# The last four output tiles of a streaming encoder's final FFN: kept weight halves and an end taken 144 frames at a time

## The chip, the cores and the metric

The kernel runs on one core of a Trainium2 chip. The metric is the device time of one execution in microseconds (us). The time before is 2776.94 us, the median of three runs (2775.93 to 2778.15). Five engines work side by side, each on its own instruction queue: PE multiplies matrices, DVE, ACT and POOL work element by element on 128 partitions, SP issues most of the DMAs.

## The reference

One inference step of a two-layer encoder on 256 prompt frames and 32 sample frames, model width 2048. Layer 0 mixes frames with a gated MLP, layer 1 with multi-scale retention; each mixer is followed by a SwiGLU FFN of hidden width 5632. Only the last lines matter here:

```python
def layer_norm(x, g, b):
    mu = jnp.mean(xf, axis=-1, keepdims=True)
    var = jnp.mean(jnp.square(xf - mu), axis=-1, keepdims=True)
    y = (xf - mu) * lax.rsqrt(var + LN_EPS) * g.astype(jnp.float32) + b.astype(jnp.float32)
...
        x = layer_norm(ALPHA * x + h, ln_mix_g[i], ln_mix_b[i])
        x = layer_norm(ALPHA * x + swiglu(x, w_ffn_in[i], w_ffn_out[i]), ln_ffn_g[i], ln_ffn_b[i])
```

The mean and the variance of one frame run over all 2048 channels. So no channel of a frame can be normalised before the last of the 16 channel tiles of that frame is known.

## The kernel before

**Layout.** Activations are held transposed: 128 channels on the partitions, the 288 frames (NT) along the free axis. A matrix of 2048 output channels is 16 output tiles `m` (KT = 16); the FFN's hidden width is 44 tiles, done in two halves of 22 (HH).

**One product in three.** Every float32 operand is split into a high part and a low part (`split`: an ACT cast, L450, then a DVE subtraction, L451). `Core.step` issues three matmuls per block of 128 x 128 weights: high weights on high data (L105), high weights on low data (L106), low weights on high data (L107), all into one PSUM bank of 288 columns. `halves` writes the access pattern of a moving operand: four elements of the second half of the frames, four of the first, and so on backwards.

**Weights.** They come from HBM in chunks of eight blocks (512 KB). `Core.prep` issues the DMA of a chunk on SP's queue into one of three `raw` buffers, casts it into one of four `whi` buffers and subtracts into one of four `wlo` buffers. A `raw` buffer is free for the next DMA when the subtraction has read it, a `whi` or `wlo` buffer when the last matmul of its chunk has read it. `Core.blk` hands out a block and calls `prep` three chunks ahead.

**Order.** PE's order is the order of the program text. DVE's and ACT's order is chosen by a planner, except inside a `manual_schedule` block with FINISH, where DVE, ACT and POOL run in the order of the text as well.

**The last stage.** `ffn` of layer 1 computes `f_out` of its second half with `Core.tiles`: output tile after output tile, 22 blocks of three matmuls each. After each tile `PostNorm.last` adds the bank to `y` (L246); `sums` subtracts a centring row (L295), squares on ACT (L297) and adds both to running sums (L300, L301). After the last tile `stats` (L307) forms mean and mean square by matmuls with a matrix of 1/2048 (L313, L316), and `finish` (L329) does the rest: variance (L373), its power -1/2 by a logarithm and an exponential on ACT (L374, L375), one Newton step (L377 to L379), then for each pair of tiles of `y` a centring and a scaling (L345; on POOL for tiles 4, 5 and 8 to 11), for four tiles a centring by PE into PSUM (L369, L370) with the scaling on DVE (L352), then the affine map with gain and bias of the channel (ACT, L362, or DVE, L360), and a store (L363). PE's constants for the centring, `ident` and `minus`, live in a `raw` buffer called `centring`, taken when 15 tiles are done.

## Time and profile before

| what | value |
|---|---|
| median of three runs | 2776.94 us |
| profiled execution, its time | 2776.59 us |
| profiled execution, its span | 2774.8 us |
| PE busy | 2762.4 us, 100% of the span |
| DVE, ACT, POOL busy | 1696.9, 1247.2, 141.6 us |

The span is the time from the first to the last instruction of the program in the profile; the run's time holds 1.8 us more. A row of the timeline gives start, duration, engine, line, operation, output and input with their shapes, and in brackets how long the engine had been idle and what ended the wait. Rows of the same kind in a row are merged ("x11" is eleven instructions). PEld is PE's weight load, which overlaps its matmuls.

### The profile page before, as it was taken

What the parts mean: (1) busy time and instruction counts of PE and PEld (TensorE: products, weight loads), DVE (VectorE), ACT (ScalarE), POOL (GpSimd) and SP (SyncE); (2) the same over time, 40 slices, a digit from 0 to 9 for tenths busy, and PEclk for the clock granted to TensorE, in tenths of its full rate; (3) what the DMA queues carried; (4) which work ended last, traced back from release to release, by engine and by line L of the source; (5) the groups of instructions that cost most, each with busy time, mean ns of one, the idle gap of its engine ahead of it and who ended that gap; (6) DMA issues with size and microseconds to landing.
All of it is one profiled execution on the core that took longest, in us unless ns stands there. A gap on an engine that the chain in (4) does not pass through costs nothing.

```text
span 2774.8 us, 51493 instructions
## 1 busy us (share of the span) xinstructions
PE 2762.4 (100%) x21590; PEld 2750.3 (99%) x21590; DVE 1696.9 (61%) x2468; ACT 1247.2 (45%) x1659; POOL 141.6 (5%) x241
## 2 busy tenths in 40 slices
PE   9999999999999999999999999999999999999998
PEld 9999999999999999999999999999999999999998
DVE  6688964445444466867765666767854455444465
ACT  5455554333343344645443444445643333333343
POOL 1100000000000000012200121210000000000001
PEclk9999999999999999999999999999999999999999
DMA  8655555555555555567765666765555555555553
GB/s 285 212 185 166 170 176 172 173 174 175 175 171 173 178 174 178 171 213 240 231 201 175 196 216 219 222 204 171 173 171 172 174 175 175 172 172 174 174 175 126
DMA packets 146585, 515.51 MB, mean 186 GB/s; under 512 B 18016, under 2 KB 20336, under 8 KB 146320
## 3 DMA queue, kind: packets, MB, share of 16 engines
q1 hardware_dynamic: 131984, 473.47, 52.6%
q0 software_dynamic: 14224, 38.59, 4.6%
q8 instruction: 169, 2.77, 0.4%
q14 instruction: 64, 0.52, 0.1%
q10 hardware_dynamic: 144, 0.15, 0.0%
HBM read 486.98 MB, written 25.17 MB: 185 GB/s over the span
## 4 chain that ended last, share of the span: by engine, by line
PE 99%; DVE 0%; DMA 0%; ACT 0%; issue 0%; SPq 0%; DVEq 0%
PE af_in L107 13%; PE af_in L105 13%; PE af_in L106 13%; PE ab_in L105 7%; PE ab_in L107 7%; PE ab_in L106 7%; PE af_out L105 6%; PE af_out L106 6%; PE af_out L107 6%; PE ab_out L105 2%; PE aa_in L106 2%; PE aa_in L105 2%; PE aa_in L107 2%; PE ab_out L107 2%; PE ab_out L106 2%; PE aa_out L106 1%
## 5 line engine op out<-in xcount | busy, mean ns | idle before, releaser
L451 DVE TENSOR_TENSOR wlo<-raw,whi 128x1024 fp32r<-128x1024 f32 (+1 forms) x892 | 1084.8, 1218 | 856.1 <-ACT whi L450 848.7
L450 ACT CAST whi<-raw 128x1024 fp32r<-128x1024 f32 (+1 forms) x892 | 933.7, 1049 | 1325.5 <-PE af_in L106 325.8
L105 PE MATMUL af_in<-xh,whi 128*128 128x288 f32 (+1 forms) x2816 | 813.3, 289 | 0.0
L107 PE MATMUL af_in<-xh,wlo 128*128 128x288 f32 (+1 forms) x2816 | 813.2, 289 | 0.0
L106 PE MATMUL af_in<-xl,whi 128*128 128x288 f32 x2816 | 811.9, 288 | 0.0
L106 PEld LDWEIGHTS af_in<-xl,whi 128*128 128x128 f32 x2816 | 528.1, 188 | 0.0
L105 PEld LDWEIGHTS af_in<-xh,whi 128*128 128x128 f32 x2816 | 528.1, 188 | 0.0
L107 PEld LDWEIGHTS af_in<-xh,wlo 128*128 128x128 f32 x2816 | 528.0, 188 | 0.0
L105 PE MATMUL ab_in<-xh,whi 128*128 128x288 f32 (+1 forms) x1536 | 445.2, 290 | 0.0
L107 PE MATMUL ab_in<-xh,wlo 128*128 128x288 f32 (+1 forms) x1536 | 444.0, 289 | 0.0
L106 PE MATMUL ab_in<-xl,whi 128*128 128x288 f32 x1536 | 443.8, 289 | 0.0
L107 PE MATMUL af_out<-hh,wlo 128*128 128x288 f32 x1408 | 406.1, 288 | 0.0
L105 PE MATMUL af_out<-hh,whi 128*128 128x288 f32 x1408 | 406.0, 288 | 0.0
L106 PE MATMUL af_out<-hl,whi 128*128 128x288 f32 x1408 | 406.0, 288 | 0.0
L106 PEld LDWEIGHTS ab_in<-xl,whi 128*128 128x128 f32 x1536 | 288.3, 188 | 0.9
L105 PEld LDWEIGHTS ab_in<-xh,whi 128*128 128x128 f32 x1536 | 288.2, 188 | 0.8
L107 PEld LDWEIGHTS ab_in<-xh,wlo 128*128 128x128 f32 x1536 | 288.2, 188 | 0.0
L105 PEld LDWEIGHTS af_out<-hh,whi 128*128 128x128 f32 x1408 | 264.0, 188 | 0.0
L107 PEld LDWEIGHTS af_out<-hh,wlo 128*128 128x128 f32 x1408 | 264.0, 188 | 0.0
L106 PEld LDWEIGHTS af_out<-hl,whi 128*128 128x128 f32 x1408 | 264.0, 188 | 0.0
L105 PE MATMUL aa_in<-xh,whi 128*128 128x288 f32 x512 | 148.1, 289 | 0.4 <-ACT xh L450 0.4
L107 PE MATMUL ab_out<-r_oh,wlo 128*128 128x288 f32 x512 | 147.8, 289 | 0.0
(248 smaller groups left out, 2915.8 us busy)
## 6 DMA issues: line engine op xcount, KB each, us to landing
raw<-in_wpack_dram SPq DMA_DIRECT2D x887, 512.0 KB, 3.4
v_room<-tv POOLq DMA_DIRECT2D x32, 144.0 KB, 4.9
of<-o_room POOLq DMA_DIRECT2D x32, 144.0 KB, 4.8
vw<-v_room POOLq DMA_DIRECT2D x8, 512.0 KB, 6.0
out_st_s_dram<-sso POOLq DMA_DIRECT2D x16, 256.0 KB, 2.7
o_room<-to POOLq DMA_DIRECT2D x8, 512.0 KB, 3.5
out_st_p_dram<-so POOLq DMA_DIRECT2D x16, 256.0 KB, 5.3
y<-in_xT_dram SPq DMA_DIRECT2D x8, 288.0 KB, 5.2
```

What stands on the lines that cost most here:

```text
L105: mm(wide, hi, halves(xh, lead), start=first, stop=False)
L106: mm(halves(ps[:, lead:], 0, lead), hi, halves(xl), start=False, stop=False)
L107: mm(wide, lo, halves(xh, lead), start=False, stop=last)
L450: nc.scalar.copy(hi, f)
L451: nc.vector.tensor_tensor(lo, f, hi.bitcast(F32), ALU.subtract)
```

## The change

It concerns the second half of layer 1's `f_out` alone, tiles 12 to 15, and the end.

- `f_out` runs through tiles 0 to 11 as before. `ending` takes tiles 12 to 15. In a first pass over these tiles it issues two matmuls of 288 columns per block: low weights on all frames of the high data, into a bank `q`, and high weights on the first 144 frames of high and of low data side by side, into a bank `p` (`paired`). So a first pass gives the first 144 frames in full and a third of the work of the other 144. `second` then issues, tile by tile, the missing matmul: high weights on the last 144 frames of high and low data.
- The high weights of these tiles are 11 chunks and stay until then: seven in the rooms of `xh` and `xl`, which layer 1's input no longer needs (`keep`), four in the `whi` buffers.
- The hidden activations' high and low parts lie in one tile `hid`, row by row, the low part 336 elements behind the high one, so that `paired` can step between them.
- `y` and the output are laid out as two halves of 144 frames.
- `ahead` centres the partial tiles 12 to 15 beforehand, and takes the `centring` buffer before the first pass rather than near its end. `stats` and `finish` are replaced for this layer by `means` and `spread`, once for each half of the frames; the power -1/2 is one ACT function of another table in place of two.
- The first half's centring, scaling, affine maps and stores are put, in the order of the text, between the `second` passes; the second half's follow after the last.

The number of matmuls of `f_out` and the bytes of weights are the same.

```diff
+NH = NT // 2
...
+ENDS = 4
+KEPT = ENDS * HH // CB
+SLOT = ROW + 16
...
-            hi = self.wp.tile([P, CB * P], F32R, tag="whi", name=f"whi{c}")
+            hi = self.keep[c] if c in self.keep else self.wp.tile([P, CB * P], F32R, tag="whi", name=f"whi{c}")
...
+def paired(x, k, h):
+
+    n = NH
+    dims = [list(x.ap[0]), [-4, n // 4], [SLOT, 2], [1, 4]]
+    v = x[:, k, h * n:]
+    return bass.AP(tensor=v.tensor, offset=v.offset + n - 4, ap=dims)
+
...
+            self.yh = y.rearrange("p k n -> p (k n)").rearrange("p (h k n) -> p h k n", h=2, n=NH)
...
+    def tile(self, m):
+        return self.y[:, m, :] if self.out is None else self.yh[:, :, m, :]
...
-                self.core.tables("natural_log_exp_and_others")
+                self.core.tables("abs_reciprocal_sqrt_and_small")
...
-    def finish(self, m1, m2):
-
-
-        nc, core, a, mean = self.nc, self.core, self.a, self.b
...
+    def ahead(self, ms):
+        nc = self.nc
+        for m in ms:
+            nc.vector.tensor_tensor(self.tile(m), self.tile(m), self.like(self.c), ALU.subtract)
+        room = self.core.wp.tile([P, CB * P], F32, tag="raw", name="centring", bufs=3)
...
+    def add(self, h, m, ps):
+        y = self.yh[:, h, m, :]
+        for o in (0, NH):
+            self.nc.vector.tensor_tensor(y, ps[:, o:o + NH], y, ALU.add)
+    def square(self, h, m):
+        self.sq = self.tmp(f"sq{h}_{m}")[:, :NH]
+        self.nc.scalar.activation(self.sq, self.yh[:, h, m, :], AF.Square)
+    def gather(self, h, m):
+        s = self.s[:, :, h * NH:(h + 1) * NH]
+        for i, d in enumerate((self.yh[:, h, m, :], self.sq)):
+            self.nc.vector.tensor_tensor(s[:, i, :], s[:, i, :], d, ALU.add)
+    def end(self, h, m, ps):
+        self.add(h, m, ps)
+        self.square(h, m)
+        self.gather(h, m)
+    def first(self, m, ps, both):
+        y = self.tile(m)
+        self.nc.vector.tensor_tensor(y, self.like(both[:, :NT]), y, ALU.add)
+        self.end(0, m, ps)
+    def means(self, h, parts):
+        core, one = self.core, self.cst["one2048"]
+        self.m = [core.bank(f"m{h}{i}")[:, :NH] for i in range(2)]
+        for j, p in enumerate(parts):
+            for m, r in zip(self.m, p):
+                self.nc.tensor.matmul(m, one, r, start=j == 0, stop=j == len(parts) - 1)
+    def sum_rows(self, h):
+        s = self.s[:, :, h * NH:(h + 1) * NH]
+        return s[:, 0, :], s[:, 1, :]
+    def spread(self, h, mids, between):
+        nc, core = self.nc, self.core
+        cols = slice(h * NH, (h + 1) * NH)
+        m1, m2 = self.m
+        self.scale, self.mean = self.a[:, cols], self.b[:, cols]
+        self.ap = ap = core.bank(f"ap{h}")[:, :NH]
+        v = core.bank(f"fin{h}")[:, :NH]
+        t, r = self.tmp(f"t{h}")[:, :NH], self.tmp(f"r{h}")[:, :NH]
+        nc.scalar.activation(t, m1, AF.Square)
+        nc.scalar.copy(self.mean, m1)
+        mids()
+        nc.vector.scalar_tensor_tensor(v, m2, LN_EPS, t, ALU.add, ALU.subtract)
+        nc.scalar.activation(r, v, AF.Abs_reciprocal_sqrt)
+        between()
+        nc.vector.scalar_tensor_tensor(ap, v, -0.5, r, ALU.mult, ALU.mult)
+        nc.vector.tensor_tensor(ap, ap, r, ALU.mult)
+        nc.vector.scalar_tensor_tensor(self.scale, ap, 1.5, r, ALU.add, ALU.mult)
+        nc.scalar.copy(ap, self.scale)
+    def rows(self, h, k, n, eng, op):
+        f = {ALU.subtract: (self.m[0], self.mean), ALU.mult: (self.ap, self.scale)}[op][eng is self.nc.gpsimd]
+        y = self.yh[:, h, k:k + n, :]
+        eng.tensor_tensor(y, y, f.unsqueeze(1).broadcast_to([P, n, NH]), op)
+    def affine(self, h, k, n, eng=None):
+        nc = self.nc
+        for i in range(k, k + n):
+            d = self.yh[:, h, i, :]
+            if eng is None:
+                nc.scalar.activation(d, d, AF.Identity, bias=self.bias(i), scale=self.gain(i))
+            else:
+                eng.tensor_scalar(d, d, self.gain(i), self.bias(i), ALU.mult, ALU.add)
+    def store(self, h, k, n, queue=None):
+        (queue or self.nc.sync).dma_start(self.out[:, h, k:k + n, :], self.yh[:, h, k:k + n, :])
+    def lift(self, h, k, n):
+        mm = self.nc.tensor.matmul
+        off = self.core.accum(f"off{k}")[:, :n * NH].rearrange("p (k n) -> p k n", n=NH)
+        for i in range(n):
+            mm(off[:, i, :], self.ident, self.yh[:, h, k + i, :], start=True, stop=False)
+            mm(off[:, i, :], self.minus, self.mean, start=False, stop=True)
+        return off
+    def ending(self, w, koff, x):
+        core, nc = self.core, self.nc
         mm = nc.tensor.matmul
+        ms = list(range(KT - ENDS, KT))
+        dve, gps = nc.vector, nc.gpsimd
+        self.ahead(ms)
+        hi, ps = {}, {}
+        for m in ms:
+            ps[m] = p, q = core.accum(f"p{m}"), core.accum(f"q{m}")
+            for k in range(HH):
+                hi[m, k], lo = core.blk(w, koff + k, m)
+                mm(halves(q), lo, halves(x[:, k, :NT]), start=k == 0, stop=k == HH - 1)
+                mm(halves(p), hi[m, k], paired(x, k, 0), start=k == 0, stop=k == HH - 1)
+            if m < KT - 1:
+                self.first(m, p, q)
+                core.tick()
+        def second(m, at={}):
+            ps[m] = b = core.accum(f"b{m}")
+            for k in range(HH):
+                mm(halves(b), hi[m, k], paired(x, k, 1), start=k == 0, stop=k == HH - 1)
+                if k in at:
+                    at[k]()
+        def quad(k, eng=dve):
+            self.rows(0, k, 4, eng, ALU.subtract)
+            self.rows(0, k, 4, eng, ALU.mult)
+        def out(k):
+            self.affine(0, k, 4)
+            self.store(0, k, 4)
         with core.tc.manual_schedule(engines=FINISH):
+            self.first(KT - 1, *ps[KT - 1])
+            second(KT - 4, {19: lambda: self.means(0, [self.sum_rows(0)])})
+            self.spread(0, lambda: None, lambda: self.rows(0, 0, 4, dve, ALU.subtract))
+            quad(12, gps)
+            self.end(1, KT - 4, ps[KT - 4])
+            self.rows(0, 0, 4, dve, ALU.mult)
+            out(0)
+            second(KT - 3)
+            quad(4)
+            out(4)
+            self.end(1, KT - 3, ps[KT - 3])
+            second(KT - 2)
+            quad(8)
+            out(8)
+            out(12)
+            self.end(1, KT - 2, ps[KT - 2])
+            second(KT - 1)
+            self.add(1, KT - 1, ps[KT - 1])
+            self.square(1, KT - 1)
+            self.means(1, [self.sum_rows(1), (self.yh[:, 1, KT - 1, :], self.sq)])
+            off = {}
+            def mids():
+                for k in (2, 5, 8):
+                    off[k] = self.lift(1, k, 3)
+                self.rows(1, 12, 4, gps, ALU.subtract)
+            self.spread(1, mids, lambda: self.rows(1, 0, 2, dve, ALU.subtract))
+            self.rows(1, 12, 4, gps, ALU.mult)
+            def lifted(k):
+                y = self.yh[:, 1, k:k + 3, :]
+                dve.tensor_tensor(y, off[k], self.scale.unsqueeze(1).broadcast_to([P, 3, NH]), ALU.mult)
+            lifted(2)
+            self.rows(1, 0, 2, dve, ALU.mult)
+            self.affine(1, 2, 3)
+            self.store(1, 2, 3)
+            lifted(5)
+            self.affine(1, 0, 2)
+            self.store(1, 0, 2)
+            lifted(8)
+            self.rows(1, 11, 1, dve, ALU.subtract)
+            self.rows(1, 11, 1, dve, ALU.mult)
+            self.affine(1, 5, 3)
+            self.store(1, 5, 3)
+            self.affine(1, 9, 3, dve)
+            self.affine(1, 8, 1)
+            self.store(1, 8, 4)
+            self.affine(1, 14, 2, dve)
+            self.affine(1, 12, 2)
+            self.store(1, 12, 4, nc.scalar)
...
+            hid = pool.tile([P, HH, 2 * ROW], F32R, name="hid")[:, :, LEAD:]
+            hh, hl = hid, hid[:, :, SLOT:]
...
+            ends = 0 if out is None or half == 0 else ENDS
+            if ends:
+                room = [t.rearrange("p k r -> p (k r)") for t in (core.wide_l, core.wide_x)]
+                for i in range(KEPT - 4):
+                    o = 56 + (i // 2) * CB * P
+                    core.keep[NCH - KEPT + i] = room[i % 2][:, o:o + CB * P]
+            core.tiles(f"f_out{layer}", half * HH, list(range(HH)), list(range(KT - ends)),
                        lambda k: (hh[:, k, :NT], hl[:, k, :NT]),
                        ln.last if half else ln.part)
+            if ends:
+                ln.ending(f"f_out{layer}", half * HH, hid)
```

More of the change, by code (lines that the diff above doesn't have):

```diff
@@ L57, in __init__ @@
         self.ready = {}
+        self.keep = {}
         self.nprep = 0
@@ L259, in last @@
             r = self.tmp("cen", F32R)
[L260 removed]
+            nc.scalar.copy(self.like(r), self.tile(m))
             self.core.after(2, lambda: self.center(r))
         self.n += 1
[L263 to L270 removed]
         if self.c is None:
@@ L278, in last @@
                 split(nc, hi, lo, self.s[:, i, :])
-        if self.n == KT:
-            self.core.after(1 if self.out is not None else 2, lambda: self.stats(m))
+            self.core.after(2, self.stats)
     def center(self, r):
@@ L312, in stats @@
             for j, r in enumerate(self.parts[i]):
-                nc.tensor.matmul(turned(st[i][:, :NT]), self.cst["one_r"], turned(r), start=j == 0, stop=j == 1 and self.out is None)
-        if self.out is not None:
-            for i, r in enumerate((self.y[:, m, :], self.sq)):
-                nc.tensor.matmul(st[i][:, :NT], one, r, start=False, stop=True)
+                nc.tensor.matmul(turned(st[i][:, :NT]), self.cst["one_r"], turned(r), start=j == 0, stop=j == 1)
         m1, m2 = st[0][:, :NT], st[1][:, :NT]
```

123 lines of the change are left out of this document (29 added, 94 removed).

## The prediction

> **What bounds the kernel now.** I read the busy shares and the chain that ended last first. PE works all the time, so only two things can move the time: PE standing still earlier, and what follows PE's last matmul.
>
> ```profile
> PE 2762.4 (100%) x21590; PEld 2750.3 (99%) x21590; DVE 1696.9 (61%) x2468; ACT 1247.2 (45%) x1659; POOL 141.6 (5%) x241
> PE 99%; DVE 0%; DMA 0%; ACT 0%; issue 0%; SPq 0%; DVEq 0%
> ```
>
> Then the timeline of the end, and the busy time by stretches (columns: stretch, its length, busy time and instructions of PE, PEld, DVE, ACT, POOL, then granted PE clock, DMA share, GB/s).
>
> ```profile
> 2757.63 0.29 PE L106 MATMUL af_out<-hl,whi 128*128 128x288 f32 x1
> 2757.76 0.29 PE L107 MATMUL af_out<-hh,wlo 128*128 128x288 f32 x1
> 2757.89 0.68 PE L313 MATMUL m<-s,one_r 128*128 128x288 f32 x4
> 2758.09 0.46 DVE L246 TENSOR_TENSOR y<-af_out,y 128x288 f32<-128x288 f32 x1 [5.48 <-PE af_out L107]
> 2758.60 0.75 PE L316 MATMUL m<-y,one 128*128 128x288 f32 x2
> 2758.64 0.44 ACT L297 ACTIVATE sq<-y 128x288 f32<-128x288 f32 x1 [6.52 <-DVE y L246]
> 2759.19 0.70 PE L316 MATMUL m<-sq,one 128*128 128x288 f32 x2
> 2759.98 0.47 DVE L373 SCALAR_TENSOR_TENSOR fin<-m,t 128x288 f32<-128x288 f32 x1 [1.44 <-PE m L316]
> 2760.48 0.41 ACT L374 ACTIVATE t<-fin 128x288 f32<-128x288 f32 x1 [0.33 <-DVE fin L373]
> 2760.93 0.44 ACT L375 ACTIVATE r<-t 128x288 f32<-128x288 f32 x1
> 2761.40 0.47 DVE L377 SCALAR_TENSOR_TENSOR ap<-fin,r 128x288 f32<-128x288 f32 x1 [0.30 <-ACT r L375]
> 2761.90 0.47 DVE L378 TENSOR_TENSOR ap<-ap,r 128x288 f32<-128x288 f32 x1
> 2762.40 0.47 DVE L379 SCALAR_TENSOR_TENSOR ap<-ap,r 128x288 f32<-128x288 f32 x1
> 2763.98 5.81 ACT L362 ACTIVATE y<-y,lnv 128x288 f32<-128x288 f32 x11
> 2767.80 2.19 DVE L360 TENSOR_SCALAR y<-y,lnv 128x288 f32<-128x288 f32 x5
> ```
>
> ```profile
> 2757.90:2763.90 6.00, 5.96 (x26) 3.99 (x24) 3.97 (x8) 2.21 (x6) 3.67 (x3) 1.00 0.00 0
> 2763.90:2768.87 4.97, 0.03 (x1) 0.00 (x0) 4.93 (x10) 4.97 (x11) 4.57 (x4) 1.00 0.48 180
> 2768.87:2774.80 5.93, 0.00 (x0) 0.00 (x0) 1.12 (x4) 0.92 (x2) 0.00 (x0) 0.50 0.69 250
> ```
>
> The reader is to see that matmuls start 0.127 us apart, that the last of `f_out` ends at 2758.05, that elementwise work ends at 2769.99 (2767.80 + 2.19), and that the span ends at 2774.8: a tail of 16.8 us, of which 4.8 us follow the last elementwise instruction. The tail is all that the change can win.
>
> **The scale.** All sums are made against the profiled execution, 2776.59 us (span 2774.8 and 1.8 around it), which is 0.35 below the median shown. I call F the end of the first pass. In the kernel before, the point 88 matmuls before the end answers to it: 2758.05 - 88 x 0.127 = 2746.9. So before, elementwise work ends at F + 23.1.
>
> **PE's work: nothing.** 4 x 22 blocks by three matmuls stay three, of 288 columns each. Added are two matmuls of means in the stream: each full-precision matmul is two passes, 0.24 apart for 288 columns (2758.60 and 2759.19 hold two each), so 0.12 for 144, and 0.5 for the four. The four L313 matmuls, 0.5 after the end, go. For `paired` reads no row exists. The nearest is L313: steps of twelve elements instead of a jump between halves, and still 0.13 each. I take 0.127; the far end is in the rivals.
>
> **Weights in the first pass: +1.5 us.** A chunk lasted 24 matmuls, 3.04 us; in the first pass it lasts 16, 2.03 us, and the same bytes must come that much faster.
>
> ```profile
> L451 DVE TENSOR_TENSOR wlo<-raw,whi 128x1024 fp32r<-128x1024 f32 (+1 forms) x892 | 1084.8, 1218 | 856.1 <-ACT whi L450 848.7
> L450 ACT CAST whi<-raw 128x1024 fp32r<-128x1024 f32 (+1 forms) x892 | 933.7, 1049 | 1325.5 <-PE af_in L106 325.8
> raw<-in_wpack_dram SPq DMA_DIRECT2D x887, 512.0 KB, 3.4
> SPq L73 <- DVE wlo L451: 121.3, 46, 6.3
> 2742.13 0.20 POOL masks.py:197 MEMSET centring<- 128x128 f32 x1 [781.98 <-DMA raw<-in_wpack_dram]
> ```
>
> A `raw` buffer's turn is 3.4 (DMA) + 1.05 (cast) + 1.22 (subtraction) + some 0.1 of hand-overs = 5.8 us; SP's queue waits for nothing but the subtraction. Three buffers give a chunk each 1.9 us, enough. But `ahead` takes one of them, `centring`, which is read to the very end; before, it was taken at 2742.1, when all weights had been asked for. Two buffers give a chunk each 2.9 us. Call the eleven chunks 0 to 10: at the first pass's start 0 to 2 are prepared, and 3 to 10 go through two buffers. Chunk 3's subtraction waits for its `wlo` buffer until the pass starts, behind two DVE instructions of tile 11 (2 x 0.46), and is done at 2.2 us. Its buffer's next turns end at 8.0 (chunk 5), 13.9 (chunk 7) and 19.8 (chunk 9). PE wants chunk 9 at 9 x 2.03 = 18.3: 1.5 late. Chunk 10, in the other buffer, is ready at 21.6, and wanted at 20.3 + 1.5. Bounds: 0, if the buffer comes back in time, and 4.0, if each of four turns waits 0.6 behind what `first` puts on DVE. I take 1.5.
>
> **The end: +1.5 us.** Durations at 144 columns come from other sizes.
>
> ```profile
> L786 DVE TENSOR_TENSOR pf<-sc,dec 128x128 f32<-128x128 f32 x8 | 2.2, 280 | 0.0
> L345 DVE TENSOR_TENSOR y<-y,ap 128x576 f32<-128x576 f32 x3 | 2.2, 746 | 0.0
> L544 ACT ACTIVATE g_vp<-g_vp,g_nrm 128x512 f32<-128x512 f32 x8 | 6.2, 802 | 0.0
> L362 ACT ACTIVATE y<-y,lnv 128x288 f32<-128x288 f32 x11 | 5.8, 618 | 0.0
> ```
>
> DVE: 0.30 for 144 columns (0.33 from one to the next that needs it), 0.75 for 576. ACT's affine map: 0.62 for 288 and 0.80 for 512, so 0.50 for 144; eleven in 5.81 start 0.52 apart, 0.10 less than they last, so 0.40 apart at 144. Halving the frames saves a quarter of each affine map, and there are 16 in the first half and 11 on ACT in the second. Bounds: 0.30 (half the other costs too) and 0.52. Square and copy: 0.30.
>
> In the order of the text, in us after F:
>
> - `first(15)`: one add of 288 and two of 144, square, sums: done at 2.0. Means start after 20 matmuls (2.5), their results are there at 3.3.
> - `spread(0)`: variance 3.7; the ACT power hides under a row subtraction (3.6 to 4.4); Newton to 5.2, copy 5.6.
> - `end(1, 12)` 5.2 to 6.5; scaling of tiles 0 to 3 to 7.1; ACT: `out(0)`, four maps, 7.2 to 8.8.
> - `quad(4)` to 8.6; `out(4)` 8.8 to 10.4. Tile 13 is added by 9.1, but its square is queued behind `out(4)`: 10.7, sums 11.0.
> - `quad(8)` to 12.4; `out(8)` and `out(12)`, eight maps, 12.5 to 15.7. Tile 14's square is queued behind them: 16.0; sums 16.3. On DVE, `add(1, 15)` is queued behind these sums: 16.9, though PE ended tile 15 at 11.8.
> - Square 17.2, means 17.6, variance 18.1, power 18.4 (one function for two), Newton 19.4, first lifted rows 20.1.
> - ACT's eleven maps from 20.1: 4.5. End 24.6. DVE ends at 24.5, PE's 18 liftings (0.25 each) at 22.4; both beside it.
>
> 24.6 against 23.1: +1.5. The stores of the first half are on SP's queue after the last weights and land under all this; for the last stores I keep 4.8. Table load: one before, one after.
>
> **POOL beside DVE: +0.4 us.**
>
> ```profile
> L360 DVE TENSOR_SCALAR y<-y,lnv x5: 418/418/829, 2767.8 to 2769.6; 128x288 f32<-128x288 f32 x5
> 2764.33 4.14 POOL L345 TENSOR_TENSOR y<-y,a 128x576 f32<-128x576 f32 x3
> ```
>
> One of the five L360 took 0.83 for 0.42: it began at 2767.80 while POOL worked until 2768.47. In the change the sums of tile 12 (5.8 on) meet POOL's scaling of the first half (5.3 to 6.7). Bounds 0 and 0.9; I take 0.4, since these are another instruction than L360. The Trainium skill, SBUF — State Buffer, section "Who interferes with whom", says that a DVE instruction with two SBUF inputs and a GpSimd instruction that reads SBUF exclude each other for a whole instruction; by that rule the sums wait to the end, the sum would have 0.9 here, 2780.5 in all.
>
> **Sum.** 1.5 + 1.5 + 0.4 = +3.4: 2780.0 us.
>
> **The rivals.**
>
> *The hiding works.* If tile 14's square and sums are not held up by the affine maps and no weight is late, add(15) starts at 11.8 and the same steps end at 20.2: 2.9 less than 23.1, 2773.7 us. For it: ACT has only some 9 us of work in these 11.8. Against it: the text's order, kept by ACT in the tail before, where the eleven L362 follow one another whatever DVE does.
>
> *PE's clock falls, slower than 0.2%.* By the order above PE has nothing but a mean's matmul (0.25 at 13.4) between F + 11.8 and 16.3. In the windows above the clock was granted in full for 4.97 us after PE's last work and 0.50 after. If the gap reaches that point, the remaining four means and 18 liftings take 0.49 instead of 0.25; liftings then end the chain, at 29.5 instead of 24.6: 2784.9 us. Against it: the gap is 4.5, with work in it. The Trainium skill, TensorE: Matmul & The Clock Gate, Part 1, puts the fall at one idle window of about 3.4 us. By that rule, counted from 11.8 and without the lone matmul, the time is that of this rival; the trace's 4.97 bears it out as a lower limit only.
>
> *The paired reads are slow.* 176 matmuls jump 336 elements rather than 144. At the 0.24 of a full-precision pass they cost 176 x 0.12 = 21 us: 2801. The even 0.127 of unlike patterns speaks against it.
>
> *Something smaller all along the stage:* `hid` moves the operands of 2112 matmuls of layer 1, 2 us for each ns; or late weights near their upper bound with maps at 0.52 (+3.2). About 2785.
>
> **How the numbers follow.** Chances: the forecast 0.50, hiding 0.16, clock 0.20, paired 0.05, the last 0.09. 0.2%, here 5.6 us, is about what a measurement of this kernel can tell from no change: 2771.4 to 2782.5. No case reaches 2771.4, so faster has 0.02. Slower gets 0.34 from the last three and 0.02 from the forecast's upper edge: 0.36. The rest, 0.62, is the same. The forecast's own range is 2776.6 (no late weight, maps at 0.30, no POOL wait: 3.4 - 1.5 - 1.5 - 0.4) to 2783. The asked range reaches down into hiding's upper half, 2775.5, and up over the clock's price, 2786; it leaves out some 0.18.
>
> **What would show it.** PE idle before the last two chunks' matmuls, with a wait on the subtraction; squares of tiles 13 and 14 behind runs of affine maps; add(15) some 5 us after PE's end; affine maps 0.40 apart. Wrong: PE's clock at 0.50 before the liftings, matmuls over 0.127 apart on `hid`, or ACT idle between `out(8)` and the square.

## The result, and the profile after

The changed kernel takes 2786.97 us, the median of six runs (2784.87 to 2788.18); the kernel before, run beside it, takes 2777.47 (2775.93 to 2779.38). The ratio is 1.0034, with a 95% interval of 1.0021 to 1.0047. So the change costs some 9.5 us: it is slower, and the predicted 2780.0 and its range, up to 2786.0, were both too low. The profiled execution took 2786.61 us with a span of 2784.8, 10.0 us longer than that of the kernel before. All sums below are made against that span. In the changed kernel's profile the three matmuls of a step are L110, L111 and L112, the first pass is L436 and L437, the second L445.

From the page: the busy shares, and the groups of f_out's matmuls by operand (busy us, mean ns of one). `hh` is layer 0, whose layout the change leaves alone; `hid` is layer 1.

```profile
PE 2771.0 (100%) x21614; PEld 2760.1 (99%) x21614; DVE 1702.9 (61%) x2497; ACT 1252.3 (45%) x1680; POOL 138.9 (5%) x239
L112 PE MATMUL af_out<-hh,wlo 128*128 128x288 f32 x704 | 203.2, 289 | 0.0
...
L111 PE MATMUL af_out<-hid,whi 128*128 128x288 f32 x616 | 179.6, 292 | 0.0
L112 PE MATMUL af_out<-hid,wlo 128*128 128x288 f32 x616 | 179.3, 291 | 0.0
L110 PE MATMUL af_out<-hid,whi 128*128 128x288 f32 x616 | 177.2, 288 | 0.0
```

PE is busy 8.6 us longer with 24 instructions more. A good part of what was lost is inside PE's busy time, where nothing looks idle: the means of L111 and L112 on `hid` are 292 and 291 ns, that of L112 on `hh` 289.

The timeline of the changed kernel, cut to the rows that answer those shown of before:

```profile
2727.58 0.29 PE L436 MATMUL q<-hid,wlo 128*128 128x288 f32 x1
2727.78 0.46 DVE L267 TENSOR_TENSOR y<-af_out,y 128x288 f32<-128x288 f32 x1 [1.76 <-PE af_out L112]
...
2745.69 0.29 PE L437 MATMUL p<-hid,whi 128*128 128x288 f32 x1
2746.22 0.40 PE L436 MATMUL q<-hid,wlo 128*128 128x288 f32 x1 [0.24 <-DVE wlo L560]
...
2748.23 0.29 PE L437 MATMUL p<-hid,whi 128*128 128x288 f32 x1
2750.33 0.40 PE L436 MATMUL q<-hid,wlo 128*128 128x288 f32 x1 [1.81 <-DVE wlo L560]
...
2753.62 1.65 PE L445 MATMUL b<-hid,xl 128*128 128x288 f32 x8
...
2759.49 1.42 POOL L401 TENSOR_TENSOR y<-y,a 128x576 f32<-128x576 f32 x1 [0.38 <-DVE a L395]
2759.94 1.14 DVE L355 TENSOR_TENSOR sums<-sums,y 128x144 f32<-128x144 f32 x1
2761.68 4.21 PE L445 MATMUL b<-hid,whi 128*128 128x288 f32 x32
2767.33 3.29 ACT L408 ACTIVATE y<-y,lnv 128x144 f32<-128x144 f32 x8 [1.83 <-DVE y L401]
2770.53 0.30 ACT L350 ACTIVATE sq<-y 128x144 f32<-128x144 f32 x1
2770.87 0.31 DVE L355 TENSOR_TENSOR sums<-sums,sq 128x144 f32<-128x144 f32 x1 [2.67 <-ACT sq L350]
2771.09 0.64 DVE L346 TENSOR_TENSOR y<-b,y 128x144 f32<-128x144 f32 x2
2775.69 0.61 DVE L490 TENSOR_TENSOR y<-off,a 128x432 f32<-128x432 f32 x1 [0.78 <-PE off L421]
2776.33 4.49 ACT L408 ACTIVATE y<-y,lnv 128x144 f32<-128x144 f32 x11 [1.05 <-DVE y L490]
2778.63 0.61 DVE L490 TENSOR_TENSOR y<-off,a 128x432 f32<-128x432 f32 x1 [0.86 <-PE off L421]
2779.70 1.41 DVE L410 TENSOR_SCALAR y<-y,lnv 128x144 f32<-128x144 f32 x5
```

And by stretches, with the columns of the prediction (PE's busy time first, the granted clock third from the end):

```profile
2747.76:2751.17 3.41, 1.60 (x12) 1.38 (x12) 1.66 (x3) 1.27 (x2) 0.00 (x0) 1.00 0.00 0
2751.18:2754.59 3.42, 3.42 (x17) 3.42 (x16) 0.83 (x3) 0.00 (x0) 0.00 (x0) 0.50 0.00 0
2764.83:2768.24 3.41, 1.06 (x9) 0.84 (x7) 2.56 (x6) 1.58 (x6) 0.00 (x0) 1.00 0.38 145
2768.24:2775.07 6.83, 4.69 (x17) 4.22 (x18) 2.44 (x8) 3.74 (x12) 1.42 (x2) 0.50 0.24 89
```

The reader is to see four losses and one gain.

1. Tile 11's addition starts at 2727.78. In the kernel before it was at 2724.64:

```profile
2724.64 0.46 DVE L246 TENSOR_TENSOR y<-af_out,y 128x288 f32<-128x288 f32 x1 [0.81 <-PE af_out L107]
```

So 3.1 us are gone before `ending` does anything.

2. The first pass lasts from 2727.58 to 2753.62, 26.0 us, where 176 matmuls at 0.127 are 22.3. Twice PE waits for `wlo`: 0.53 and 2.10 from one matmul to the next, and the first matmul behind each wait is 0.24 from the second. Against 0.127 each, that is 0.40 + 1.97 + 2 x 0.11 = 2.6 us. Then the granted clock is at 0.50 from 2751.18 on, and the last ten matmuls of the pass start 0.24 apart: 1.1 us.

3. The last elementwise instruction ends at 2779.70 + 1.41 = 2781.1, that is F + 27.5 with F = 2753.62. Before, it was F + 23.1 by the prediction's F, the end of a matmul; by the start of the next one, as F is taken here, it would be F + 23.3.

4. The granted clock is at 0.50 a second time, from 2768.24 to 2775.07, just while the second half's means and half of its liftings run.

The gain: what follows the last elementwise instruction takes 3.7 us instead of 4.8. In sum 3.1 + 3.7 + 4.4 - 1.1 = 10.1, against 10.0 measured.

### The profile page after: what moved, and what is told of

Same layout as the page of the kernel before. It is cut to its first block, busy times and chain, and to the rows that moved or that the text cites. A ratio compares the mean times of both kernels' runs of the same rounds, so it can differ in the third digit from the quotient of the medians.

```text
span 2784.8 us, 51601 instructions
## 1 busy us (share of the span) xinstructions
PE 2771.0 (100%) x21614; PEld 2760.1 (99%) x21614; DVE 1702.9 (61%) x2497; ACT 1252.3 (45%) x1680; POOL 138.9 (5%) x239
## 4 chain that ended last, share of the span: by engine, by line
PE 98%; DVE 1%; DMA 1%; ACT 0%; issue 0%; DVEq 0%; POOL 0%; ACTq 0%; POOLq 0%
PE af_in L110 13%; PE af_in L112 13%; PE af_in L111 13%; PE ab_in L110 7%; PE ab_in L112 7%; PE ab_in L111 7%; PE af_out L111 6%; PE af_out L112 6%; PE af_out L110 6%; PE aa_in L112 2%; PE aa_in L110 2%; PE aa_in L111 2%; PE ab_out L110 2%; PE ab_out L111 2%; PE ab_out L112 2%; PE aa_out L111 1%
## 5 line engine op out<-in xcount | busy, mean ns | idle before, releaser
L110 PE MATMUL af_in<-xh,whi 128*128 128x288 f32 (+1 forms) x2816 | 814.1, 289 | 0.0
L112 PE MATMUL af_in<-xh,wlo 128*128 128x288 f32 (+1 forms) x2816 | 813.8, 289 | 0.0
L111 PE MATMUL af_in<-xl,whi 128*128 128x288 f32 x2816 | 812.8, 289 | 0.0
L111 PEld LDWEIGHTS af_in<-xl,whi 128*128 128x128 f32 x2816 | 528.6, 188 | 0.0
L112 PEld LDWEIGHTS af_in<-xh,wlo 128*128 128x128 f32 x2816 | 528.6, 188 | 0.0
L110 PEld LDWEIGHTS af_in<-xh,whi 128*128 128x128 f32 x2816 | 528.4, 188 | 0.0
L110 PE MATMUL ab_in<-xh,whi 128*128 128x288 f32 (+1 forms) x1536 | 445.4, 290 | 0.0
L112 PE MATMUL ab_in<-xh,wlo 128*128 128x288 f32 (+1 forms) x1536 | 444.0, 289 | 0.0
L111 PE MATMUL ab_in<-xl,whi 128*128 128x288 f32 x1536 | 444.0, 289 | 0.0
L111 PEld LDWEIGHTS ab_in<-xl,whi 128*128 128x128 f32 x1536 | 288.4, 188 | 0.9
L110 PEld LDWEIGHTS ab_in<-xh,whi 128*128 128x128 f32 x1536 | 288.2, 188 | 0.8
L112 PEld LDWEIGHTS ab_in<-xh,wlo 128*128 128x128 f32 x1536 | 288.4, 188 | 0.0
L112 PE MATMUL af_out<-hh,wlo 128*128 128x288 f32 x704 | 203.2, 289 | 0.0
L110 PE MATMUL af_out<-hh,whi 128*128 128x288 f32 x704 | 203.2, 289 | 0.0
L111 PE MATMUL af_out<-hl,whi 128*128 128x288 f32 x704 | 203.2, 289 | 0.0
L111 PE MATMUL af_out<-hid,whi 128*128 128x288 f32 x616 | 179.6, 292 | 0.0
L112 PE MATMUL af_out<-hid,wlo 128*128 128x288 f32 x616 | 179.3, 291 | 0.0
L110 PE MATMUL af_out<-hid,whi 128*128 128x288 f32 x616 | 177.2, 288 | 0.0
L110 PE MATMUL aa_in<-xh,whi 128*128 128x288 f32 x512 | 148.4, 290 | 0.0
L112 PE MATMUL ab_out<-r_oh,wlo 128*128 128x288 f32 x512 | 147.8, 289 | 0.0
```

Source lines behind the costliest of these rows:

```text
L110: mm(wide, hi, halves(xh, lead), start=first, stop=False)
L111: mm(halves(ps[:, lead:], 0, lead), hi, halves(xl), start=False, stop=False)
L112: mm(wide, lo, halves(xh, lead), start=False, stop=last)
```

## The experiments

Ratios are to the kernel before, run beside each; the span is that of the profiled execution. Different executions of one kernel lie up to 5.5 us apart (2781.28 to 2786.79 for the one with two sums ahead of the maps), so the traces, not the medians, carry the readings of single microseconds.

| kernel | median us | runs | ratio, 95% interval | span us |
|---|---|---|---|---|
| changed kernel | 2786.97 | 6 | 1.0034 [1.0021, 1.0047] | 2784.8 |
| before, `hid` layout alone | 2779.65 | 10 | 1.0011 [1.0002, 1.0021] | 2777.7 |
| constants in their own tile | 2783.55 | 8 | 1.0024 [1.0013, 1.0034] | 2782.3 |
| two sums ahead of the maps | 2783.35 | 10 | 1.0023 [1.0014, 1.0033] | 2780.4 |
| two blocks, 28224 B apart | 2785.99 | 5 | 1.0034 [1.0021, 1.0047] | 2784.1 |
| two blocks, 28160 B apart | 2783.51 | 10 | 1.0018 [1.0009, 1.0028] | 2778.8 |
| two blocks, 28192 B apart | 2781.67 | 10 | 1.0020 [1.0011, 1.0029] | 2779.8 |
| one matmul added per half | 2782.62 | 10 | 1.0020 [1.0010, 1.0029] | 2780.6 |
| PE kept busy | 2783.52 | 10 | 1.0021 [1.0011, 1.0030] | 2782.9 |
| without POOL's first rows | 2783.58 | 8 | 1.0025 [1.0014, 1.0035] | 2785.0 |
| second order of the end | 2778.74 | 10 | 1.0007 [0.9998, 1.0017] | 2776.1 |
| third order of the end | 2778.08 | 10 | 1.0006 [0.9997, 1.0016] | 2776.0 |
| all together | 2774.43 | 11 | 0.9990 [0.9981, 0.9999] | 2772.3 |

### Where the hidden activations lie

*The kernel before with nothing but the layout of `hid`*, the 176 B of `shift_hid` ahead of it included, which the changed kernel has too:

```diff
-        hh = moving(pool, HH, f"hh{layer}")
-        hl = moving(pool, HH, f"hl{layer}")
...
+            pool.tile([P, 44], F32, name="shift_hid")
+            hid = pool.tile([P, HH, 2 * ROW], F32R, name="hid")[:, :, LEAD:]
+            hh, hl = hid, hid[:, :, ROW + 16:]
```

> The kernel before with one part of the change alone: the hidden activations of layer 1 lie in one tile, row by row, the low part 336 elements behind the high one. Theory (layout): the 616 + 616 + 616 matmuls of f_out on this tile run at 128.9 ns instead of 126.7 until PE is interrupted, as in the trace after, so some 2.3 to 3.1 us more than before: about 2780. Rival (the kept weights or the paired reads cause the beat): no change, 2777, and 126.7 ns throughout.

The beat of f_out (the mean distance of two starts) can be counted in one stretch of 100 us of its first half. The row of before, that of the changed kernel, and that of this one:

```profile
2240.00:2340.00 100.00, 100.00 (x791) 100.00 (x790) 51.26 (x60) 34.69 (x33) 0.00 (x0) 1.00 0.53 174
```

```profile
2240.00:2340.00 100.00, 100.00 (x778) 100.00 (x777) 50.97 (x59) 33.62 (x32) 0.00 (x0) 1.00 0.51 170
```

```profile
2240.00:2340.00 100.00, 100.00 (x778) 100.00 (x777) 50.78 (x59) 33.80 (x32) 0.00 (x0) 1.00 0.49 169
```

In the same 100 us 791 matmuls are touched before and 778 with the layout, at the same granted clock and with PE never idle. From the starts themselves: 126.67 ns before, 128.89 ns in both others, through all 1056 matmuls of the half, 2.35 us. In the second half the slow beat holds only up to the centring row's matmul (2668.9 us in the changed kernel, 2668.6 in this one); behind it the same addresses run at 126.67. So the loss there is 0.7 us, and 3.05 of the 3.1 us come with the layout alone, without `ending`. Which part of the layout does it, the distance, the longer rows or the place, this run does not separate.

*The changed kernel with `hh` and `hl` in two blocks again*, `SLOT` elements apart, here 28224 B. The two kernels after it differ from this one in `SLOT` alone: `HH * ROW` (28160 B, the distance in the kernel before) and `HH * ROW + 8` (28192 B).

```diff
-            hid = pool.tile([P, HH, 2 * ROW], F32R, name="hid")[:, :, LEAD:]
-            hh, hl = hid, hid[:, :, SLOT:]
+            both = pool.tile([P, SLOT + HH * ROW], F32R, name="hid")
+            hh, hl = (both[:, o:o + HH * ROW].rearrange("p (k r) -> p k r", r=ROW)[:, :, LEAD:] for o in (0, SLOT))
+            hid = hh
...
-SLOT = ROW + 16
+SLOT = HH * ROW + 16
```

> The change with the high and the low parts of the hidden activations in two blocks of their own, row length 320 as before, the low block 7056 elements behind the high one, so paired jumps 7056 elements. Theory (layout): f_out back at 126.7 ns, 3.1 us less than after, 2784. Rival (the beat comes from the long jump or the kept weights): no change, 2787; or, if long jumps are slow in themselves, the 176 paired matmuls take longer than 127 ns each.

> The changed kernel with hh and hl in two separate blocks again, row 320, hl 28160 B behind hh as in the kernel before (so both at the kernel before's addresses); the paired reads step over 28160 B, an even multiple of 64 B. Offset theory (the slow beat of layer 1's f_out comes with an hl that lies an odd multiple of 64 B behind hh): both halves of f_out back at 126.7 ns a matmul, tile 11's add near 2724.6 us as before, the paired matmuls of the end still near 127 ns, so about 2783.8 us (3.1 less than the changed kernel). Rival A (the beat comes from other addresses or from the ending's code): f_out stays near 129 ns, about 2786. Rival B (paired reads at an even multiple of 64 B are slow): f_out fast, but the 176 paired matmuls of the end well above 127 ns; at twice the time 11 us for each half, about 2806.

> As the kernel with hl 28160 B behind hh, but 28192 B (8 elements more, half of 64 B beyond an even multiple). Two prices are asked for at once, that of f_out (126.7 ns at 28160 B, 130 ns at 28224 B) and that of a paired matmul in the second half (148 ns at 28160 B, 126.7 to 133 ns at 28224 B and 1344 B). If only a whole odd multiple of 64 B upsets f_out and only a whole even multiple upsets the paired reads: 126.7 ns for both, about 2782. If the paired reads want an odd multiple: 148 ns again, about 2783.5. If any pad upsets f_out: 129 to 130 ns, about 2786.

The same stretch of the three, at 28224, 28160 and 28192 B:

```profile
2240.00:2340.00 100.00, 100.00 (x772) 100.00 (x771) 50.52 (x59) 33.67 (x32) 0.00 (x0) 1.00 0.49 169
```

```profile
2240.00:2340.00 100.00, 100.00 (x792) 100.00 (x791) 51.79 (x60) 34.73 (x33) 0.00 (x0) 1.00 0.51 174
```

```profile
2240.00:2340.00 100.00, 100.00 (x787) 100.00 (x786) 50.70 (x60) 34.75 (x33) 0.00 (x0) 1.00 0.48 173
```

And 8 us of the second pass, whose matmuls read paired, at 28160 and at 28192 B:

```profile
2752.00:2760.00 8.00, 8.00 (x56) 8.00 (x56) 6.53 (x16) 4.41 (x12) 2.78 (x2) 1.00 0.10 37
```

```profile
2752.00:2760.00 8.00, 8.00 (x66) 8.00 (x65) 6.61 (x15) 4.50 (x14) 2.85 (x2) 1.00 0.09 34
```

Measured between starts, f_out's beat in the first half is 130.0 ns at 28224 B, 126.67 at 28160 B and 127.4 at 28192 B, with `hh` at one place in all three. So two blocks by themselves do not bring the beat back, as had been expected at 28224 B; moving `hl`, and with it what lies behind it, is enough to change it. The paired reads go the other way: 56 matmuls instead of 66 at 28160 B, that is 146 to 148 ns instead of 127 (133 at 28224 B). That is the rival "the paired reads are slow", at some 20 ns each and not 120; the changed kernel's 1344 B avoids it, and pays at f_out. 28192 B has nearly the best of both, 127.4 and 127, as the first of its three expectations had it, but for a rest of 0.75 ns in f_out.

*One matmul more in each half*, nothing else changed:

```diff
+            if out is not None:
+                def flip():
+                    o = core.bank(f"flip{half}")
+                    nc.tensor.matmul(turned(o[:, :NT]), cst["one_r"], turned(hh[:, 0, :NT]), start=True, stop=True)
+
+                core.after(1, flip)
             core.tiles(f"f_out{layer}", half * HH, list(range(HH)), list(range(KT - ends)),
```

> The changed kernel, its layout of hid untouched, with one matmul more in each half of layer 1's f_out, some 8.5 us after the half begins (the constant one_r against a row group of hh, into a bank that nobody reads). Theory of two beats (the same addresses run in either beat, and an interruption sets which: the one at 2666 us in half 1 was followed by 126.7 ns): f_out runs at about 129 ns up to the added matmul and at 126.7 ns behind it, 2.2 us less in half 0 and 0.5 us in half 1, tile 11's add near 2725.0 us, time about 2784.2. Rival (the addresses alone hold half 0 in the slow beat): 129 ns goes on behind the added matmul, tile 11's add near 2727.9, time about 2787.

```profile
2240.00:2340.00 100.00, 100.00 (x792) 100.00 (x791) 51.22 (x60) 34.83 (x33) 0.00 (x0) 1.00 0.49 174
```

In the first half the theory of two beats holds: 128.9 up to the added matmul, 126.67 behind it, with `hid` where it was; 2.07 us less. In the second half it was too simple: the matmuls run at 127.7 ns from the start of the half, ahead of its own added matmul, and at 127.8 behind it and behind the centring row, where the changed kernel had 128.89 and then 126.67. So this half is 0.27 us longer than without the added matmul. There are more than two beats, and which one runs depends on the addresses and on what ran before. Why, no run shows.

### The weights of the first pass

*The centring constants in a tile of their own*, so that `ahead` takes no `raw` buffer:

```diff
             if ends:
+                ln.spare = pool.tile([P, 2 * P], F32, name="centring")
...
-        room = self.core.wp.tile([P, CB * P], F32, tag="raw", name="centring", bufs=3)
+        room = self.spare
```

> The change with the centring constants in 1 KB of their own, so that the weights keep three raw buffers in the first pass. Theory (buffer): the two gaps of 0.4 and 2.0 us in the first pass go, and with them the fall of PE's clock at 2751 to 2755 (some 2 us): about 4.5 us less than after, 2782.5. Rival (the memory is the limit: 512 KB in 2.03 us are 258 GB/s): the gaps stay, at most 0.5 us less, 2786.5.

PE's waits in the first pass and the end (us in total, times, the longest), of the changed kernel and then of this one, and this one's first pass by stretch:

```profile
PE m L372 <- DVE sums L355: 4.5, 2, 2.4
PE q L436 <- DVE wlo L560: 2.1, 2, 1.8
```

```profile
PE m L372 <- DVE sums L355: 4.8, 2, 2.5
```

```profile
2728.00:2750.30 22.30, 22.30 (x178) 22.30 (x178) 15.71 (x27) 7.55 (x10) 0.00 (x0) 1.00 0.39 138
```

The waits for `wlo` are gone, PE is busy throughout, and the clock does not fall in this pass. The cause is the buffer, as predicted; HBM, asked for the same bytes in the same time, keeps up, although single transfers take up to 4.6 us here.

What the waits come to differs from one execution to the next. The transfer of the last chunk, by the view of DMA issues (KB each, us to landing), in the changed kernel and in the kernel with two sums ahead of the maps, which has the two buffers too:

```profile
raw<-in_wpack_dram SPq DMA_DIRECT2D x1, 512.0 KB, 4.6
```

```profile
raw<-in_wpack_dram SPq DMA_DIRECT2D x1, 512.0 KB, 3.1
```

In the first PE lost 1.97 us at this chunk, in the second 0.1. Among the eight traces with two buffers, transfers of 4.6 to 4.9 us go with 1.8 to 2.1 us lost there (four traces), those of 3.1 to 3.6 us with at most 0.3 (the other four). Why the last transfer is sometimes longer, no run shows. The clock fell in this pass in the changed kernel's trace alone.

### The queues of the end, and the clock

*Two of the second half's sums ahead of the first half's maps:*

```diff
-            out(4)
             self.end(1, KT - 3, ps[KT - 3])
+            out(4)
             second(KT - 2)
             quad(8)
-            out(8)
-            out(12)
             self.end(1, KT - 2, ps[KT - 2])
+            out(8)
+            out(12)
             second(KT - 1)
```

> The change with the squares and sums of tiles 13 and 14 put ahead of the first half's affine maps in the text. Theory (queue): add(1,15) starts right after PE's end, some 3 to 4 us earlier, PE is not idle long enough for its clock to fall before the means: 3.5 to 5 us less than after, about 2783. Rival (DVE is full, the squares only move the wait): under 1 us less, 2786.

```profile
2763.10 0.93 PE L372 MATMUL m<-sums,one 128*128 128x144 f32 x4 [1.25 <-DVE sums L355]
...
2766.57 0.84 PE L372 MATMUL m<-sq,one 128*128 128x144 f32 x2 [1.98 <-ACT sq L350]
```

The expected time came, 2783 us, but not the expected full clock. The queue has moved on by one: now tile 15's square stands behind `out(8)` and `out(12)`. PE waits for the square instead of the sums, 1.98 us, and the clock falls at 2765.4. The span is 4.4 us shorter all the same, part of it because the first pass's waits came out shorter in this execution (0.4 us in place of 2.1, by the view of waits).

*PE kept busy while it waits*, with nine more of the first half's pairs of means ahead of the second half's:

```diff
+            self.means(1, 9 * [self.sum_rows(0)])
             self.means(1, [self.sum_rows(1), (self.yh[:, 1, KT - 1, :], self.sq)])
```

> The changed kernel with 36 more matmul passes (the first half's sums once more, nine times, into the bank that the second half's means then overwrite), put between the last paired matmul and the second half's means, where TensorE waited 5 us. Clock theory: no fall at 2768.2 us, means and liftings at 113 ns a pass instead of 240, first lifted rows 1.5 to 2 us earlier, span 1.5 to 2 us shorter (near 2783), time near 2785. Rival (ScalarE's queue alone sets the end, the half clock is hidden by it): under 0.5 us, near 2786.7.

```profile
2765.08 4.82 PE L372 MATMUL m<-sums,one 128*128 128x144 f32 x38
2770.58 0.51 PE L372 MATMUL m<-sums,one 128*128 128x144 f32 x2 [0.68 <-DVE sums L355]
```

The useless matmuls delay nothing, and the clock stays at 1.00 to the end of the liftings. From the start of `t` (the first ACT instruction behind the means) to the last elementwise instruction it takes 2771.75 to 2779.28, 7.5 us; the kernel without POOL's rows, whose queues are alike and whose clock falls, takes 9.1 (2772.26 to 2781.32), 1.5 us more. In the changed kernel, whose clock is back sooner, it is 8.4 (2772.74 to 2781.11), and 0.3 more is lost between tile 15's square and `t` (0.97 against 0.63): there the second fall costs 1.2 us.

*Without POOL's rows of the first 144 frames* (`quad(12, gps)` taken out):

> The changed kernel without POOL's centring and scaling of rows 12 to 15 of the first 144 frames (left out, so these rows are stored unnormalised). Contention theory: VectorE's sum of tile 12 of the second half takes 0.31 us instead of 1.135, and what follows it on VectorE starts 0.8 us earlier. Whether the end gains is open: 0.8 us if VectorE's chain carries it (near 2786.1), nothing if ScalarE's maps do. Rival (the sum is slow for another reason, say its wait on the square): it stays near 1.1 us.

```profile
2760.09 0.31 DVE L355 TENSOR_TENSOR sums<-sums,y 128x144 f32<-128x144 f32 x1
```

0.31 where it was 1.14. Tile 15's square comes 17.05 us after the first pass (2771.29 - 2754.24) against 17.69 (2771.12 - 2753.43) where PE was kept busy, 0.64 less: most of POOL's price travels down the queues to the end.

*The second order.* The sums of tiles 13, 14 and 15 come first, the maps of `out(4)` stand two and two behind them, and `quad(8)`, `out(8)` and `out(12)` go into the waits of `spread(1)`; the constants have their own tile. In this kernel rows 8 to 11 of the first 144 frames meet the second half's mean and scale in place of their own.

```diff
             quad(4)
-            out(4)
             self.end(1, KT - 3, ps[KT - 3])
+            self.affine(0, 4, 2)
             second(KT - 2)
-            quad(8)
-            out(8)
-            out(12)
             self.end(1, KT - 2, ps[KT - 2])
+            self.affine(0, 6, 2)
+            self.store(0, 4, 4)
             second(KT - 1)
...
```

> The changed kernel with the centring constants in a tile of their own, and the end's queues in another order: the sums of tiles 13, 14, 15 of the second 144 frames ahead of the first 144 frames' later quads on VectorE and ScalarE; these quads fill the waits of the second half's statistics. Queue theory (the last square waited behind up to twelve maps of ScalarE, TensorE then stood idle and its clock fell): square of tile 15 about 1 us after TensorE's last paired matmul instead of 5, TensorE idle under 1.5 us, the liftings at 0.113 ns a column pass (113 ns each) rather than 240 ns, last elementwise instruction near first pass + 21.5 us instead of 27.6; span near 2776, time about 2778. Rival (the work itself, ScalarE's 27 maps and VectorE's rows, bounds the end whatever the order): last elementwise at 26 after the first pass, about 2782 to 2783.5 as with the constants alone.

```profile
2760.99 0.88 PE L372 MATMUL m<-sums,one 128*128 128x144 f32 x4
...
2763.91 0.48 PE L423 MATMUL off<-b,centring 128*128 128x144 f32 x2 [0.83 <-ACT b L389]
2766.51 6.08 ACT L410 ACTIVATE y<-y,lnv 128x144 f32<-128x144 f32 x15 [0.82 <-DVE y L403]
```

PE goes from the second pass, whose last matmul starts at 2760.86, into the means at once (2760.99), the liftings run at full clock, and the last elementwise instruction ends 23.3 us after the first pass, with 15 maps of ACT in a row as the last stretch. The queue theory holds; 21.5 had left these maps out.

*The third order:* rows 8 to 11 go to POOL behind rows 12 to 15, with their own mean and scale, and their maps to DVE while PE forms the means.

```diff
             quad(12, gps)
+            quad(8, gps)
...
+            def early():
+                self.affine(0, 8, 4, dve)
+                self.store(0, 8, 4)
+                self.affine(0, 12, 2)
...
```

> As the kernel with the other order of the end's queues and the centring constants in a tile of their own, now with rows 8 to 11 of the first 144 frames on POOL behind its rows 12 to 15 (with the first half's mean and scale) and their maps on VectorE while TensorE forms the second half's means. Queue theory: ScalarE has eleven maps left behind the second half's scale where it had fifteen, so the last elementwise instruction comes near first pass + 21.5 us instead of 23.3, span near 2774.5, time near 2776.5. Rival (VectorE or POOL takes the place of ScalarE, through sums slowed beside POOL): no gain, 2778 to 2779.

```profile
2756.93 1.53 DVE L355 TENSOR_TENSOR sums<-sums,sq 128x144 f32<-128x144 f32 x1
```

ACT has eleven maps left, as meant, but now the second sum of tile 12 is caught behind POOL as well, 1.53 us for 0.31: the rival, and no gain that could be told. In the trace the last elementwise instruction does come sooner, at F + 22.4, but this execution began its first pass 0.7 us later (2727.72 against 2727.04).

*All together:* the third order with tile 12's, 13's and 14's sums taken out from between the additions and put behind them, when POOL is done with these rows; the constants' own tile; the added matmul.

```diff
...
+            def front(m):
+                self.add(1, m, ps[m])
+                self.square(1, m)
+                sq[m] = self.sq
...
+            for m in ms[:3]:
+                self.sq = sq[m]
+                self.gather(1, m)
             self.add(1, KT - 1, ps[KT - 1])
...
```

> What the runs so far point to, together: the changed kernel with the centring constants in a tile of their own, the added matmul in each half of layer 1's f_out, and a third order of the end: VectorE adds tiles 12, 13 and 14 of the second 144 frames first, and forms their sums (the instructions that slow down beside POOL) only behind them, when POOL has done its eight rows of the first 144 frames. By the terms measured one by one: the last order's span 2776.0, less 2.9 for the beat, less some 1.5 for sums that POOL no longer slows (0.84 and 1.2 us there): span near 2771.6, time near 2773.6, ratio to the kernel before 0.9987, no interruption of the first pass, and full clock until the liftings are done. Rival (the gains overlap, the end being held by ScalarE's maps): span 2773 to 2774, time 2775 to 2776, no difference from the kernel before that can be told.

By stretches: the first pass, the second, means and liftings, the last maps.

```profile
2725.70:2748.00 22.30, 22.30 (x178) 22.30 (x177) 15.54 (x27) 8.61 (x11) 0.00 (x0) 1.00 0.42 138
2748.00:2759.80 11.80, 11.80 (x96) 11.80 (x95) 8.57 (x25) 5.63 (x16) 5.68 (x4) 1.00 0.07 26
2759.80:2765.50 5.70, 5.41 (x41) 4.89 (x40) 4.96 (x14) 4.31 (x13) 2.81 (x2) 1.00 0.41 155
2765.50:2768.60 3.10, 0.68 (x6) 0.46 (x4) 2.35 (x8) 3.01 (x8) 0.00 (x0) 1.00 0.47 171
```

2774.43 us, ratio 0.9990 with an interval that ends at 0.9999: faster than the kernel before by what these runs can only just tell. With both passes free of waits, full clock and no sum beside POOL, the last elementwise instruction comes at F + 20.7 (2768.70 - 2748.00). So the idea of the change can gain some 2.5 us of span (2772.3 against 2774.8); the changed kernel's way of doing it lies 12.5 above that, at 2784.8.

## Why the prediction was wrong

The failed step is "PE's work: nothing": 3.1 us. The second is the full clock on which the sum rests, put into a rival: 2.8 us. The waits of the first pass were mis-sized.

- **PE's work: nothing.** The counting of matmuls was right, the price of one was not. The 1848 matmuls on `hid` ahead of `ending` cost 3.1 us more, because of where `hid` lies. The last rival named exactly this ("`hid` moves the operands of 2112 matmuls of layer 1, 2 us for each ns"), at a chance that went by no row. The kernel before could not show what the new addresses would cost, but it does show that 0.127 is not the only beat: 312 matmuls are touched in this stretch, 128.9 ns each, and 318 in the 40 us from 2020 on, at 126.67.

```profile
1960.00:2000.00 40.00, 40.00 (x312) 40.00 (x311) 38.56 (x72) 27.57 (x41) 0.15 (x1) 1.00 0.53 171
```

- **Weights in the first pass: +1.5.** The mechanism was right (the buffer that `centring` holds), the term mis-sized: 2.6 us of waits, plus 1.1 that the term did not have, since the waits brought the clock down. The prediction had chunk 9 late by 1.5 and chunk 10 in time. Chunk 9 cost 0.40 and chunk 10 1.97, the latter because its transfer took 4.6 us where 3.4 was taken for all. In the two traces in which it took 3.1 (two sums ahead; 28192 B) the waits came to 0.7 and 1.0, below the term.
- **The end: +1.5.** The chain came as written up to add(15): tile 13's square stands behind `out(4)`, tile 14's behind `out(8)` and `out(12)`, add(15) at 2771.09 when PE's last paired matmul started at about 2765.6; affine maps 0.40 apart (3.29 us for eight that last 0.49); eleven of them in 4.49 us for 4.5. Add(15) was done 18.1 us after F for the predicted 16.9: POOL put 0.64 on that, the half clock in the second pass's first matmuls some 0.46 (tile 15's square came 18.15 us after F here, 17.69 with full clock), which leaves 0.1. From there to the last elementwise instruction it took 9.4 us for the predicted 7.7. The second fall of the clock is 1.2 of that, and 0.5 is left with full clock too (8.2 where PE was kept busy). What ended last was VectorE behind PE's liftings, not ScalarE's maps: the third lifted rows, at 2778.63, waited 0.86 us for PE, and the maps were done 0.3 us ahead of VectorE's.
- **POOL beside DVE: +0.4.** The sum took 0.83 longer, and 0.64 reached the end. By the exclusion rule of the Trainium skill, SBUF — State Buffer, section "Who interferes with whom", the prediction had an estimate of 0.9. The trace agrees: the sum that starts at 2759.94 ends just behind POOL's instruction of 2759.49 (2761.07 and 2760.91), though it is another instruction than L360.
- **PE's clock falls.** Held to be a rival at 0.20, and it came twice, for 1.1 and 0.5 us around the first pass's end, where no rival had it, and for 1.2 at the end. "Against it: the gap is 4.5, with work in it" was the wrong argument. What counted, by the stretches shown, was the share of a stretch of 3.41 us: 1.60 us busy of it, and the clock fell; 1.06 busy, and it fell again. Its price was overrated: the prediction took half clock for all means and liftings (4.9 us), but the clock was back at 2775.07.
- **Last stores: 4.8 kept.** 3.7 were measured. Before, the last store was issued 0.44 us behind the last elementwise instruction and took 3.12 to land, with four other stores on their way (DMA share 1.02 from 2770 to 2772); here it was issued 0.07 behind and took 2.30.
- **The paired reads** run at 127 ns in the changed kernel, as taken. That this hangs on `SLOT` came out only when `SLOT` was changed.

Of 10.0 us, then, the prediction had 1.5 of 3.7 in the first pass and 1.9 of 4.4 at the end, nothing of the 3.1 of the layout, and missed the 1.1 gained at the stores.

## What to carry to other kernels

A changed address is a changed operand: when a layout moves under thousands of matmuls, count their starts in one long stretch before and after, since PE looks fully busy in both. Where an engine runs its instructions in the order of the text, what a late stage needs must stand ahead of what merely has to be done some time, and moving it up by one place only hands the wait on to the next in the queue. A wait of two microseconds of PE costs more than itself if it leaves too little work in a stretch of 3.4 us; work that was already waiting can be put there, even useless work.

## What the runs showed of the hardware

- The beat of equal matmuls at full granted clock takes several values, by operand addresses and by history: 126.67, 127.4, 127.8, 128.9 and 130.0 ns were seen on f_out of layer 1. One matmul in between can set another one (128.9 to 126.67 in the first half). The kernel before has it too, in other stages (128.9 from 1960 to 2000 us). The mechanism is open.
- A moving operand that steps by four elements between two blocks costs 127 ns a matmul at 1344 B and 28192 B, 133 at 28224 B, and 146 to 148 at 28160 B.
- The clock's falls last 3.41 or 6.83 us in the traces where it rose again. A stretch of that length with 1.60 us of work brought it down, while in the kernel without POOL's rows nearly the same wait, cut otherwise, left 1.70 and did not:

```profile
2748.69:2752.10 3.41, 1.70 (x14) 1.47 (x12) 1.28 (x2) 1.27 (x2) 0.00 (x0) 1.00 0.01 1
2752.10:2755.50 3.40, 3.40 (x26) 3.40 (x27) 1.43 (x5) 0.00 (x0) 0.00 (x0) 1.00 0.00 0
```

The Trainium skill, TensorE: Matmul & The Clock Gate, Part 1, has a free-running window of 3413 ns and lets the clock fall after an idle one. The length agrees with these traces; "idle" is too narrow, as 1.60 us of 3.41 busy was not enough. Where the limit lies is not settled: two other stretches, placed by the edges of the falls, with 42% (third order, from 2768.45) and 46% of their time busy (28224 B, from 2764.10), were followed by full clock, and one with 42% (two sums ahead, from 2762.00) by half.
